# State reads and outputs of the SSD branch moved in front of adaLN units, with outputs cut into four column strips

## The chip, the cores and the metric

The kernel runs on one core of one Trainium2 chip. The metric is the device time of one execution in microseconds (us); less is better. All times below come from the hardware profiler's record of one execution, or from timed runs.

## The reference, cut to what matters

One layer of a decoder runs on 256 prompt tokens and 8 x 8 sample tokens (320 columns in all). The part that the change touches is the SSD branch (Mamba-2), in 8 groups of 8 heads:

```
cs = cumsum(dt * A)
cb = einsum('btgn,bsgn->btsg', C, B)               # products of one group
w  = cb * exp(cs_t - cs_s) * dt                     # weights, masked to s <= t
y  = einsum('btsgh,bsghp->btghp', w, x)             # outputs
y += exp(cs) * einsum('btgn,bghpn->btghp', C, h0)   # read of the old state h0
h  = exp(cs_last) * h0 + einsum('bsgh,bsghp,bsgn->bghpn', dL, x, B)   # new state
y  = rmsnorm_group((y + d_skip * x) * silu(z)) * ssd_norm
```

Beside it the adaLN modulation is computed: `mod = silu(c) @ w_ada`, for 9 rows (1 prompt, 8 samples), 12288 columns wide.

## The kernel before, in words

Every large product is a GEMM with fp32 weights that are split in two parts (`whi` by ScalarE at line 132, `wlo` by VectorE at line 106); a block of it is three TensorE matmuls (`hi*hi`, `lo*hi`, `hi*lo`) over 320 columns, called `mm` in the profile. `quad_mm` runs one quad, that is 512 x 512 weights: 2 halves of 4 output blocks (`mb`), 6 matmuls per block. The blocks of one GEMM lie in four PSUM banks (tag `mm`, 4 buffers), so the next GEMM's block takes the bank of the same block of the GEMM before it, once that has been evacuated.

TensorE's order is the order in which the program is written; the other engines get theirs from a scheduler when the program is built, and each engine then works strictly in that order. Two kinds of small work are put between the blocks:

- **Background generators.** `bg.tick()` is called after every block (8 times in a quad). A generator yields how many ticks it wants to skip. `ssd_work` is the one that matters: for each group it transposes B and x, reads the 8 sample states with `C` (`inter`: 4 matmuls for each half `hf`, each on a strip of 32 columns of the array, four strips side by side), updates the states (`upd`), makes the products (`cb`), token-major x (`xT`, then `xdt`), the weights (`w`: three Relu and one Exp on ScalarE, a product on GpSimd), the outputs (`y`: 8 matmuls for each of 4 steps `j`, on two strips of 64 columns), and the prompt's final state (`fin`). The decay rows `csb` (two loads of 640 KB) feed the weights.
- **adaLN units.** `ada.mm()` stands behind every second quad (`ada_every`). A unit is 4 matmuls on four strips of 32 columns (`ad`); when the unit before it closed a column block, `flush` first puts 4 transposes (`p`) in front of it.

One group takes, in this order: a GEMM for `xs` (with the convolution), one for the gate `z` (its four blocks go through a Silu on ScalarE in `evac_z`), then 4 GEMMs of one quad each for the projection of the group before (`w_sp`; evacuated by VectorE into `yb`). `ssd_work` begins when `z` begins: tick 16 is the end of z's second quad, tick 32 the end of z, tick 48 and 64 the ends of the second and fourth quads of the projection. An adaLN unit stands behind each of these four.

Before the change the generator goes by tick counts alone: the first read is at tick 16, the second at tick 26, the outputs at ticks 52, 57, 62 and 67. Both `csb` loads and four state loads are issued at tick 16.

Of the kernel before, what the change touches and what calls it, by code (L numbers as in the profile page):

```python
# [19 lines left out]
NT = 320  # L20
# [40 lines left out]
def hybrid_kernel(tc, ctx, a, o):  # L61
# [71 lines left out]
        return first, tt(eng, lo, src, hi.bitcast(F32), ALU.subtract)  # L133


    class Background:
        def __init__(self):
            self.queue = []
# [2 lines left out]
        def add(self, gen):  # L141
            self.queue.append(gen)

        def tick(self):
            if self.wait > 0:
                self.wait -= 1
                return
            if self.queue:
                try:
                    self.wait = next(self.queue[0]) or 0  # L150
                except StopIteration:
                    self.queue.pop(0)
# [95 lines left out]
    class Ada:  # L248
# [23 lines left out]
                self.loaded.append((c, b0, nb, q, raws))  # L272

        def mm(self):
            self.flush()
            if not self.loaded:
                return
            c, b0, nb, q, raws = self.loaded.pop(0)
            if q == 0:
                t = psum.tile([128, 512], F32, tag="ad", bufs=1, name="ad")  # L280
                self.ps = t
            w = 128 * nb
            m = 2048 // w
            n = m // len(raws)
            for j in range(m):
                T.matmul(self.ps[32 * (j % 4):32 * (j % 4) + 32, :w], c_s[:, m * q + j, :],
                         raws[j // n][:, (j % n) * w:(j % n) * w + w], start=q == 0 and j < 4,
                         stop=q == nb - 1 and j >= m - 4, tile_position=(0, 32 * (j % 4)))
            if q == nb - 1:
                part = stile([128, 512], name="adap")  # L290
                S.copy(part[:, :w], self.ps[:, :w])  # L291
                self.parts.append((c, b0, nb, part))
# [31 lines left out]
        T.matmul(ps, wh, xl, start=False, stop=False)  # L324
        T.matmul(ps, wl, xh, start=False, stop=stop)

    def quad_mm(pss, name, xq, first, last, evac, n_ada, apart, later):
        xh, xl = xq
        if n_ada:
            ada.load()  # L330
        for h in range(2):
            wh, wl = stream.take(name + (h,))
            for mb in range(4):
                for k2 in range(2):
                    kk = 2 * h + k2
                    c = k2 * 512 + mb * 128
                    block(pss[mb][:, :NT], wh[:, c:c + 128], wl[:, c:c + 128],
                          xh[:, kk], xl[:, kk], first and kk == 0, last and kk == 3)
                if mb == 0:
                    stream.ahead(1 if apart and last and h == 1 else S_AHEAD)  # L340
                if h == 0 and mb == 1 and later is not None:
                    later()
                if last and h == 1 and evac is not None:
                    evac(mb, pss)
                bg.tick()
        if n_ada:
            ada.mm()

# [3 lines left out]
    def gemm(names, quads, evac, apart=False):  # L352
        pss = [mm_ps() for _ in range(4)]
        n = len(names)
        for q in range(n):
            quad_no[0] += 1
            xq = quads(q) if callable(quads) else quads[q]
            quad_mm(pss, names[q], xq, q == 0, q == n - 1, evac,
                    1 if ada_every[0] and len(ada.units) > 4 and quad_no[0] % ada_every[0] == 0 else 0, apart,
                    (lambda: quads(q + 1)) if callable(quads) and q + 1 < n else None)  # L360


# [611 lines left out]
    def v8(x):  # L974
        return x.rearrange("p (h d) -> p h d", d=64)
# [4 lines left out]
    def ssd_work(W):  # L980
# [19 lines left out]
        xl = stile([64, 512], name="xl")  # L1000
        tt(V, v8(xl), v8(ps[0:64]), bc8(dtL_tok[:, hsl]), ALU.mult)
        tt(V, v8(xs_tok[0:64]), v8(ps[0:64]), bc8(dt_tok[0:64, 2, hsl]), ALU.mult)
        yield 4

        psA = ax_ps("inter")
        for hf in range(2):
            mv = stack_v(xl, hf)
            states.read(psA, [cpad[:, 4 * hf + j] for j in range(4)], hf, hf == 0, hf == 1)
            for j in range(4):
                st = states.tiles[4 * hf + j]  # L1010
                tt(G, v8(st), v8(st), bc8(ecs_all[:, hsl, 4 * hf + j]), ALU.mult)
            if hf == 0:
                csb = []
                for i in range(2):
                    t = qtile(name="csb")
                    src = bass.AP(tensor=cs_d.tensor, offset=cs_d.offset + (8 * g + 4 * i) * NT,
                                  ap=[[0, 128], [NT, 4], [1, NT]])
                    now(nc.sync.dma_start(t, src))
                    csb.append(t)
            yield 1  # L1020
            for j in range(4):
                states.update(hf, j, hst[hf][:, j], mv, lambda st, ps: tt(V, st, st, ps, ALU.add))
                yield 1
        inter = stile([128, 512], name="inter")
        tt(V, v8(inter), v8(psA), bc8(ecs_r[:, hsl]), ALU.mult)
        yield 1
        states.store(8)

        ps = ax_ps("cb")
        T.matmul(ps[:, 0:256], Bc[:, 0:128], Cc[:, 0:256], start=True, stop=True)  # L1030
        T.matmul(ps[:, 256:384], Bc[:, 128:256], Cc[:, 128:256], start=True, stop=True)
        wide = W.bcm.rearrange("p a b -> p (a b)")[:, NT * 2 * (g % 2) + NP:NT * 2 * (g % 2) + NP + 128]
        T.matmul(ps[:, 384:448], wide, Cc[:, 256:320], start=True, stop=True)
        cb = stile([128, 448], name="cb")
        tt(V, cb[:, 0:384], ps[:, 0:384], mask[:, 0:384], ALU.mult)
        tt(V, cb[0:64, 384:448], ps[0:64, 384:448], mask[0:64, 384:448], ALU.mult)

        wt = ws[0:64]
        for i in range(2):
            now(tt(V, wt[:, 4 * i:4 * i + 4], csb[i][0:64, :, NP:],  # L1040
                   cs_tok[0:64, 2, 8 * g + 4 * i:8 * g + 4 * i + 4].unsqueeze(2).to_broadcast([64, 4, 64]),
                   ALU.subtract))
        V.tensor_scalar(out=wt, in0=wt, scalar1=0.0, scalar2=None, op0=ALU.min)
        act(wt, wt, AF.Exp)
        tt(V, wt, wt, cb[0:64, 384:448].unsqueeze(1).to_broadcast([64, 8, 64]), ALU.mult)
        yield

        xdt = []
        for tb in range(2):
            ps = ax_ps("xT")  # L1050
            for mb in range(4):
                T.transpose(ps[:, 128 * mb:128 * mb + 128], xs[:, mb, 128 * tb:128 * tb + 128], ident)
            xt = stile([128, 512], name="xdt")
            tt(V, v8(xt), v8(ps), bc8(dt_tok[:, tb, hsl]), ALU.mult)
            xdt.append(xt)
            yield

        ps = ax_ps("bT")
        for tb in range(2):
            T.transpose(ps[:, 128 * tb:128 * tb + 128], Bc[:, 128 * tb:128 * tb + 128], ident)  # L1060
        bt = stile([128, 2, 128], name="bt")
        S.copy(bt, ps[:, 0:256].rearrange("p (a b) -> p a b", a=2))
        xL = []
        for tb in range(2):
            xl = stile([128, 512], name="xL")
            tt(G, v8(xl), v8(xdt[tb]), bc8(dL_tok[:, tb, hsl]), ALU.mult)
            xL.append(xl)
        yield 3
        ps = ax_ps("fin")
        for tb in range(2):  # L1070
            T.matmul(ps, bt[:, tb], xL[tb], start=tb == 0, stop=tb == 1)
            yield
        fs = stile([128, 512], name="fs")
        S.copy(fs, ps)
        nc.sync.dma_start(o["ssm_p"][g], fs)


        def weights(h):
            cbr = csb[h // 4][:, h % 4]
# [6 lines left out]
            tt(G, w, w, cb[:, 0:384], ALU.mult)  # L1086
            return w

        ahead = [weights(0), weights(1)]
        yield 4  # L1090
        for j in range(4):
            if j < 3:
                ahead += [weights(2 * j + 2), weights(2 * j + 3)]

            ps = ax_ps("y")
            w = [ahead.pop(0), ahead.pop(0)]
            for cols, lhs, rhs, first in (
                    (slice(0, 256), xdt[0], lambda e: w[e][:, 0:256], True),
                    (slice(128, 256), xdt[1], lambda e: w[e][:, 256:384], False),
                    (slice(256, 320), xs_tok, lambda e: ws[:, 2 * j + e], True),  # L1100
                    (slice(256, 320), inter, lambda e: sel, False)):
                for e in range(2):
                    h = 2 * j + e
                    T.matmul(ps[64 * e:64 * e + 64, cols], lhs[:, 64 * h:64 * h + 64], rhs(e), start=first,
                             stop=not first, tile_position=(0, 64 * e))
            i = 4 * g + j
            V.scalar_tensor_tensor(out=xs[:, j], in0=xs[:, j], scalar=vec[:, V_DS + i:V_DS + i + 1],
                                   in1=ps[:, :NT], op0=ALU.mult, op1=ALU.add)
            yield 4

    def ssd_finish(W):
        g, xs = W.g, W.xs
# [332 lines left out]
```

## Time and profile before

| | |
|---|---|
| median of 3 runs | 2912.64 us (2911.92 to 2913.28) |
| the profiled execution | 2912.8 us |
| its span, first to last instruction | 2910.7 us |
| TensorE matmuls busy | 2863.7 us, 98% of the span |
| VectorE, ScalarE, GpSimd busy | 1587.1, 1239.2, 378.3 us |
| SSD outputs (`y`) | from 726.9 to 1587.1 us of the span |

The span is 2.1 us shorter than the execution's own time. Matmul rows give a start, a length and a count; matmuls overlap, so what a stretch costs is read from starts: while only `mm` run, one starts every 0.147 us. "[0.98 <-DVE st L106]" behind a row is the time for which the engine was idle before it and the work that ended this.

### The profile page before, as it was taken

The page shows a single profiled execution, that of the slowest core. Times are in us where ns is not written, and L with a number is a line of the kernel's source. Part 1 is how long each engine was busy: PE and PEld are TensorE (multiplying, and loading weights), DVE is VectorE, ACT ScalarE, POOL GpSimd, SP SyncE. Part 2 cuts the span into 40 slices and gives each one's busy share as a digit, 9 for nine tenths or more (in the row PEclk, how much of TensorE's full clock was granted, in tenths as well). Part 3 has the DMA queues.
Part 4 walks back from the last instruction along what each step waited for, and adds up shares of the span by engine and source line. Part 5 has one row for each costly group of instructions (what it writes and reads, how often), then busy time and mean ns, then how long its engine had stood idle before and what let it go on. Part 6 is the DMA issues. An engine that isn't in the chain of part 4 may idle for free.

```text
span 2910.7 us, 48455 instructions
## 1 busy us (share of the span) xinstructions
PE 2863.7 (98%) x19596; PEld 2683.9 (92%) x19596; DVE 1587.1 (55%) x2302; ACT 1239.2 (43%) x1955; POOL 378.3 (13%) x517
## 2 busy tenths in 40 slices
PE   7999999999999999999999999999999999999998
PEld 5889999988889989889888999999999999999998
DVE  5666555666646666666665544456444444443445
ACT  4354544344454554445454333335333233333333
POOL 0012021123223232323232000000000000000000
PEclk9999999999999999999999999999999999999999
DMA  9855755747666676775767544554444444444443
GB/s 385 320 171 190 243 170 192 244 143 274 224 236 238 204 259 198 254 240 200 259 200 253 196 168 157 170 206 150 148 152 149 149 152 151 147 152 150 148 151 116
DMA packets 181111, 575.54 MB, mean 198 GB/s; under 512 B 23252, under 2 KB 24600, under 8 KB 180888
## 3 DMA queue, kind: packets, MB, share of 16 engines
q1 hardware_dynamic: 180888, 572.45, 57.8%
q8 instruction: 154, 2.52, 0.3%
q14 instruction: 69, 0.57, 0.1%
HBM read 528.63 MB, written 43.74 MB: 197 GB/s over the span
## 4 chain that ended last, share of the span: by engine, by line
PE 50%; DVE 1%; ACT 0%; issue 0%; DVEq 0%
PE mm L115 49%; PE ad L115 0%; DVE x L106 0%; PE y L115 0%; PE sum L115 0%; DVE x L1193 0%; PE upd L115 0%; PE fin L115 0%; PE inter L115 0%; PE xT L118 0%; PE p L118 0%; DVE ss L106 0%; PE cb L115 0%; DVE rt L106 0%; ACT adap L291 0%
## 5 line engine op out<-in xcount | busy, mean ns | idle before, releaser
L106 DVE TENSOR_TENSOR wlo<-raw,whi 128x1024 fp32r<-128x1024 f32 x712 | 884.3, 1244 | 949.6 <-ACT whi L132 946.5
L132 ACT CAST whi<-raw 128x1024 fp32r<-128x1024 f32 x712 | 745.7, 1048 | 1366.5 <-PE mm L115 1032.7
L115 PE MATMUL mm<-hh,whi 128*128 128x320 f32 x2560 | 817.6, 319 | 8.7 <-ACT u L946 6.7
L115 PE MATMUL mm<-hh,wlo 128*128 128x320 f32 x2560 | 793.2, 310 | 0.8 <-DVE wlo L106 0.8
L115 PE MATMUL mm<-hl,whi 128*128 128x320 f32 x2560 | 792.4, 310 | 1.3 <-DVE hl L106 1.3
L115 PEld LDWEIGHTS mm<-hh,whi 128*128 128x128 f32 x2560 | 482.9, 189 | 89.4 <-issue 42.5
L115 PEld LDWEIGHTS mm<-hl,whi 128*128 128x128 f32 x2560 | 483.3, 189 | 11.1 <-issue 3.8
L115 PEld LDWEIGHTS mm<-hh,wlo 128*128 128x128 f32 x2560 | 482.8, 189 | 1.4 <-DVE wlo L106 1.3
L115 PE MATMUL mm<-gh,whi 128*128 128x320 f32 x1408 | 435.3, 309 | 0.8 <-ACT gh L1267 0.8
L115 PE MATMUL mm<-gl,whi 128*128 128x320 f32 x1408 | 435.4, 309 | 0.0
L115 PE MATMUL mm<-gh,wlo 128*128 128x320 f32 x1408 | 435.1, 309 | 0.0
L115 PEld LDWEIGHTS mm<-gh,whi 128*128 128x128 f32 x1408 | 264.3, 188 | 1.8 <-ACT gh L1267 1.8
L115 PEld LDWEIGHTS mm<-gl,whi 128*128 128x128 f32 x1408 | 264.3, 188 | 0.5 <-DVE gl L106 0.3
L115 PEld LDWEIGHTS mm<-gh,wlo 128*128 128x128 f32 x1408 | 264.3, 188 | 0.0
L115 PE MATMUL mm<-ahi,whi 128*128 128x320 f32 x704 | 217.5, 309 | 0.0
L115 PE MATMUL mm<-alo,whi 128*128 128x320 f32 x704 | 217.5, 309 | 0.0
L115 PE MATMUL mm<-ahi,wlo 128*128 128x320 f32 x704 | 217.5, 309 | 0.0
L106 POOL TENSOR_TENSOR ss<-ss,sq 128x320 f32<-128x320 f32 x14 | 12.8, 912 | 1401.9 <-ACT sq L109 1401.8
L115 PE MATMUL mm<-yhi,whi 128*128 128x320 f32 x512 | 170.2, 332 | 0.0
L115 PE MATMUL mm<-yhi,wlo 128*128 128x320 f32 x512 | 158.4, 309 | 0.6 <-DVE wlo L106 0.6
L115 PE MATMUL mm<-ylo,whi 128*128 128x320 f32 x512 | 158.0, 309 | 0.0
L115 PEld LDWEIGHTS mm<-ahi,whi 128*128 128x128 f32 x704 | 132.1, 188 | 0.0
(281 smaller groups left out, 3616.0 us busy)
## 6 DMA issues: line engine op xcount, KB each, us to landing
raw<-w_in SPq DMA_DIRECT2D x320, 512.0 KB, 4.1
raw<-w_fi SPq DMA_DIRECT2D x176, 512.0 KB, 3.3
raw<-w_ada SPq DMA_DIRECT2D x120, 512.0 KB, 5.7
raw<-w_fo SPq DMA_DIRECT2D x88, 512.0 KB, 3.4
raw<-w_sp SPq DMA_DIRECT2D x64, 512.0 KB, 5.3
araw<-w_ada SPq DMA_DIRECT2D x52, 512.0 KB, 8.5
st<-S_gla SPq DMA_DIRECT2D x64, 256.0 KB, 5.1
gla_s<-st SPq DMA_DIRECT2D x64, 256.0 KB, 4.6
```

Source lines behind the costliest of these rows:

```text
L106: return eng.tensor_tensor(out=out, in0=in0, in1=in1, op=op)
L115: Tensor.last = nc.tensor.matmul(*args, **kw)
L132: first = S.copy(hi, src)
```

## The change

A tick that stands right in front of an adaLN unit is now marked as such (`unit`), and a generator can yield `UNIT` to skip to it. In `ssd_work` both state reads and the outputs (two steps `j` together) wait for such a tick: ticks 16, 32, 48 and 64. An output matmul is cut into two of 32 columns, so that one step is 16 matmuls over four strips. `ada.mm` runs its unit first and the transposes of the block before it afterwards. The products `cb`, the token-major x and the first two heads' weights stand between the two reads (ticks 24 to 29), the sample weights and heads 2 and 3 at tick 42, heads 4 to 7 behind the first outputs. `fin` stands behind the first outputs. States 4 to 7 are loaded at tick 13, `csb` at ticks 20 and 32.

```diff
+    UNIT = "unit"
...
-        def tick(self):
-            if self.wait > 0:
+        def tick(self, unit=False):
+            if self.wait == UNIT and not unit:
+                return
+            if self.wait != UNIT and self.wait > 0:
                 self.wait -= 1
                 return
...
         def mm(self):
+            old, self.parts = self.parts, []
+            self.unit()
+            new, self.parts = self.parts, old
             self.flush()
+            self.parts = new
...
-    def quad_mm(pss, name, xq, first, last, evac, n_ada, apart, later):
+    def quad_mm(pss, name, xq, first, last, evac, slot, apart, later):
+        n_ada = slot and len(ada.units) > 4
...
-                bg.tick()
+                bg.tick(h == 1 and mb == 3 and slot)
...
+        mv = stack_v(xl, 0)
+        yield 1
+        states.load(8)
+        yield UNIT
+        psA = ax_ps("inter")
+        for hf in range(2):
+            states.read(psA, [cpad[:, 4 * hf + j] for j in range(4)], hf, hf == 0, hf == 1)
+            for j in range(4):
+                st = states.tiles[4 * hf + j]
+                tt(G, v8(st), v8(st), bc8(ecs_all[:, hsl, 4 * hf + j]), ALU.mult)
+            if hf == 1:
+                decay_rows(1)
+            yield 1
+            for j in range(4):
+                if hf == 0 and j == 1:
+                    decay_rows(0)
+                states.update(hf, j, hst[hf][:, j], mv, lambda st, ps: tt(V, st, st, ps, ALU.add))
+                if j < 3:
+                    yield 1
+            if hf == 0:
+                cb = products()
+                yield 1
+                for tb in range(2):
+                    token_major(tb)
+                    yield tb
+                ahead += [weights(h) for h in range(2)]
+                mv = stack_v(xl, 1)
+                yield UNIT
...
+        states.store(8)
+        sample_weights()
+        ahead += [weights(h) for h in range(2, 4)]
...
+        for p in range(2):
+            yield UNIT
+            for j in (2 * p, 2 * p + 1):
...
+                    for e in range(2):
+                        for c in (0, 32):
+                            at = 64 * e + c
+                            T.matmul(ps[at:at + 32, cols], lhs[:, 128 * j + at:128 * j + at + 32], rhs(e),
+                                     start=first, stop=not first, tile_position=(0, at))
...
+            if p == 0:
+                ahead += [weights(h) for h in range(4, 8)]
+                yield 3
```

On TensorE, this is an output step of the last group before the change (`w` on `xdt`, `ws` and `inter` are its operands), alone between blocks of the projection:

```order
L115 MATMUL mm<-yhi,wlo 128x320
L115 MATMUL y<-w,xdt 64x256 x2
L115 MATMUL y<-w,xdt 64x128 x2
L115 MATMUL y<-ws,xs_tok 64x64 x2
L115 MATMUL y<-cst,inter 64x64 x2
L115 MATMUL mm<-yhi,whi 128x320
```

And the last outputs of the same group in the changed program, two steps and the unit:

```order
L115 MATMUL mm<-yhi,wlo 128x320
L115 MATMUL y<-w,xdt 32x256 x4
L115 MATMUL y<-w,xdt 32x128 x4
L115 MATMUL y<-ws,xs_tok 32x64 x4
L115 MATMUL y<-cst,inter 32x64 x4
L115 MATMUL y<-w,xdt 32x256 x4
L115 MATMUL y<-w,xdt 32x128 x4
L115 MATMUL y<-ws,xs_tok 32x64 x4
L115 MATMUL y<-cst,inter 32x64 x4
L115 MATMUL ad<-raw,c_s 32x512 x4
L115 MATMUL mm<-hh,whi 128x320
```

Four lone steps became two pairs, and each pair touches a unit; a step has twice the matmuls.

On ScalarE, this is the end of the z GEMM in the seventh group before the change (`z<-mm` are the four Silu evacuations, `whi` the weight casts, `adap` a unit's result):

```order
L132 CAST whi<-raw 128x1024 x2
L109 ACTIVATE z<-mm 128x320 x2
L132 CAST whi<-raw 128x1024
L109 ACTIVATE z<-mm 128x320 x2
L132 CAST whi<-raw 128x1024
L291 COPY adap<-ad 128x512
L132 CAST whi<-raw 128x1024 x2
L109 ACT_TABLE_LOAD
L109 ACTIVATE ws<-ws 64x512
```

And the same place in the changed program (`w` are the weights of heads 0 and 1):

```order
L132 CAST whi<-raw 128x1024
L109 ACTIVATE z<-mm 128x320
L109 ACTIVATE w<-csb,cs_tok 128x128
L109 ACTIVATE w<-csb,nd_tok 128x128
L109 ACTIVATE w<-csb,cs_tok 128x128 x2
L109 ACT_TABLE_LOAD
L109 ACTIVATE w<-w 128x384
...
L519 CAST mv<-xl 32x512
L109 ACTIVATE w<-w 128x384
L109 ACT_TABLE_LOAD
L109 ACTIVATE z<-mm 128x320 x3
L301 COPY adap<-ad 128x512
```

The work for two heads' weights, with a table load at either end, now stands between the first and the second Silu of z. The order is the same in all 8 groups. In the whole program ScalarE has 61 table loads, 45 before.

On VectorE, the same group in the changed program between its two reads; `st` is a state's addition of `upd`, which frees the bank that `upd` wrote:

```order
L106 TENSOR_TENSOR st<-st,upd 128x512
L106 TENSOR_TENSOR wlo<-raw,whi 128x1024
L106 TENSOR_TENSOR st<-st,upd 128x512
L106 TENSOR_TENSOR wlo<-raw,whi 128x1024
L106 TENSOR_TENSOR st<-st,upd 128x512 x2
L106 TENSOR_TENSOR cb<-cb,cst 128x384
```

Before the change no `wlo` stands between the four `st` of this read, and `cb` comes after the second read's.

## Rows read from the trace of the kernel before

**Rows 1.** The page, busy time of each engine (share of span, instructions).
```profile
PE 2863.7 (98%) x19596; PEld 2683.9 (92%) x19596; DVE 1587.1 (55%) x2302; ACT 1239.2 (43%) x1955; POOL 378.3 (13%) x517
```
**Rows 2.** Chain that ended last, in order of time: start, us, what.
```profile
1433.90 1.76 PE mm L115 x12
...
1457.09 0.44 PE p L118 x4
```
**Rows 3.** Timeline of TensorE around a lone state read (left out) at 1430.64.
```profile
1430.40 0.31 PE L115 MATMUL mm<-hh,wlo 128*128 128x320 f32 x1
...
1431.89 0.30 PE L115 MATMUL mm<-hl,whi 128*128 128x320 f32 x1
```
**Rows 4.** Timeline of TensorE, a state read with a unit right behind it.
```profile
1418.03 0.31 PE L115 MATMUL mm<-hh,wlo 128*128 128x320 f32 x1
1418.27 1.06 PE L115 MATMUL inter<-st,cpad 128*32 128x512 f32 x8
1419.15 1.04 PE L115 MATMUL ad<-raw,c_s 128*32 128x512 f32 x8
...
1420.37 0.31 PE L115 MATMUL mm<-hl,whi 128*128 128x320 f32 x1
```
**Rows 5.** Timeline of TensorE: read, four transposes and unit between these two.
```profile
1524.28 0.31 PE L115 MATMUL mm<-hh,wlo 128*128 128x320 f32 x1
...
1527.35 0.31 PE L115 MATMUL mm<-hl,whi 128*128 128x320 f32 x1
```
**Rows 6.** Timeline of TensorE, one output step on two strips.
```profile
1461.92 0.31 PE L115 MATMUL mm<-yhi,wlo 128*128 128x320 f32 x1
...
1462.86 0.28 PE L115 MATMUL y<-ws,xs_tok 128*64 128x64 f32 x4
1462.97 0.29 PE L115 MATMUL y<-cst,inter 128*64 128x64 f32 x4
...
1463.45 0.31 PE L115 MATMUL mm<-ylo,whi 128*128 128x320 f32 x1
```
**Rows 7.** Timeline of ScalarE, a cast and the Silu of z behind it.
```profile
1436.03 1.04 ACT L132 CAST whi<-raw 128x1024 fp32r<-128x1024 f32 x1
1436.97 0.44 ACT L109 ACTIVATE z<-mm 128x320 f32<-128x320 f32 x1
```
**Rows 8.** Timeline of ScalarE, a copy for `mv`; Relus and Exp of weights.
```profile
1419.69 0.62 ACT L508 CAST mv<-xl 32x512 fp32r<-32x512 f32 x1
...
1455.84 0.41 ACT L109 ACTIVATE w<-csb,cs_tok 128x128 f32<-128x128 f32 x1
...
1457.02 0.51 ACT L109 ACTIVATE w<-w 128x384 f32<-128x384 f32 x1
```
**Rows 9.** Timeline of ScalarE, a table load between a cast and Silus.
```profile
776.79 1.05 ACT L132 CAST whi<-raw 128x1024 fp32r<-128x1024 f32 x1 [2.31 <-DMA raw<-w_in]
777.86 1.28 ACT L109 ACT_TABLE_LOAD   x1
779.15 1.02 ACT L109 ACTIVATE xs<-cacc 128x256 f32<-128x256 f32 x4
```
**Rows 10.** Timeline of TensorE, first block behind a late evacuation.
```profile
632.50 0.64 PE L115 MATMUL mm<-hh,whi 128*128 128x320 f32 x1 [6.66 <-ACT u L946]
```
**Rows 11.** Groups by line and shape, `upd`: busy, mean ns, idle before.
```profile
L115 PE MATMUL upd<-mv,hs 96*128 96x512 f32 x128 | 52.4, 410 | 4.0 <-DVE st L106 2.6 <-DVE mv L106 1.1 <-DVE st L670 0.3
```
**Rows 12.** Stretches: us, TensorE busy (instructions), granted clock, DMA share, GB/s.
```profile
210.95:214.39 3.44, 2.34 (x11) 1.00 1.02 375
214.39:217.80 3.41, 3.41 (x13) 0.50 0.63 205
...
796.50:799.90 3.40, 2.42 (x17) 1.00 1.05 405
798.80:802.20 3.40, 3.39 (x22) 1.00 0.99 358
```
**Rows 13.** Who waited for whom: total us, times, longest.
```profile
ACT whi L132 <- DMA raw<-w_sp: 44.6, 35, 4.4
```

More of the change, by code (lines that the diff above doesn't have):

```diff
@@ L274, in mm, with unit @@
         def mm(self):
+            old, self.parts = self.parts, []
+            self.unit()
+            new, self.parts = self.parts, old
             self.flush()
+            self.parts = new
+        def unit(self):
             if not self.loaded:
@@ L358, in gemm @@
             quad_mm(pss, names[q], xq, q == 0, q == n - 1, evac,
-                    1 if ada_every[0] and len(ada.units) > 4 and quad_no[0] % ada_every[0] == 0 else 0, apart,
+                    ada_every[0] > 0 and quad_no[0] % ada_every[0] == 0, apart,
                     (lambda: quads(q + 1)) if callable(quads) and q + 1 < n else None)
@@ L1002, in ssd_work @@
         tt(V, v8(xs_tok[0:64]), v8(ps[0:64]), bc8(dt_tok[0:64, 2, hsl]), ALU.mult)
[L1003 to L1049, printed above, removed]
+        csb, xdt, ahead = [], [], []
+        def products():
+            ps = ax_ps("cb")
+            T.matmul(ps[:, 0:256], Bc[:, 0:128], Cc[:, 0:256], start=True, stop=True)
+            T.matmul(ps[:, 256:384], Bc[:, 128:256], Cc[:, 128:256], start=True, stop=True)
+            wide = W.bcm.rearrange("p a b -> p (a b)")[:, NT * 2 * (g % 2) + NP:NT * 2 * (g % 2) + NP + 128]
+            T.matmul(ps[:, 384:448], wide, Cc[:, 256:320], start=True, stop=True)
+            cb = stile([128, 448], name="cb")
+            tt(V, cb[:, 0:384], ps[:, 0:384], mask[:, 0:384], ALU.mult)
+            tt(V, cb[0:64, 384:448], ps[0:64, 384:448], mask[0:64, 384:448], ALU.mult)
+            return cb
@@ new lines, in sample_weights @@
+        def sample_weights():
+            wt = ws[0:64]
+            for i in range(2):
+                now(tt(V, wt[:, 4 * i:4 * i + 4], csb[i][0:64, :, NP:],
+                       cs_tok[0:64, 2, 8 * g + 4 * i:8 * g + 4 * i + 4].unsqueeze(2).to_broadcast([64, 4, 64]),
+                       ALU.subtract))
+            V.tensor_scalar(out=wt, in0=wt, scalar1=0.0, scalar2=None, op0=ALU.min)
+            act(wt, wt, AF.Exp)
+            tt(V, wt, wt, cb[0:64, 384:448].unsqueeze(1).to_broadcast([64, 8, 64]), ALU.mult)
@@ L1050, in ssd_work, with token_major @@
+        def token_major(tb):
             ps = ax_ps("xT")
@@ L1055, in ssd_work, with weights, decay_rows @@
             xdt.append(xt)
-            yield
+        def weights(h):
+            cbr = csb[h // 4][:, h % 4]
+            hh = 8 * g + h
+            w = pool.tile([128, 384], F32, tag="w", bufs=4, name="w")
+            now(act(w[:, 0:128], cbr[:, 0:128], AF.Relu, scale=-1.0, bias=cs_tok[:, 0, hh:hh + 1]))
+            now(act(w[:, 128:256], cbr[:, 128:256], AF.Relu, scale=-1.0, bias=nd_tok[:, hh:hh + 1]))
+            now(act(w[:, 256:384], cbr[:, 128:256], AF.Relu, scale=-1.0, bias=cs_tok[:, 1, hh:hh + 1]))
+            act(w, w, AF.Exp, scale=-1.0)
+            tt(G, w, w, cb[:, 0:384], ALU.mult)
+            return w
+        def decay_rows(i):
+            t = qtile(name="csb")
+            src = bass.AP(tensor=cs_d.tensor, offset=cs_d.offset + (8 * g + 4 * i) * NT,
+                          ap=[[0, 128], [NT, 4], [1, NT]])
+            now(nc.sync.dma_start(t, src))
+            csb.append(t)
+        mv = stack_v(xl, 0)
[26 more added lines that the diff above has]
+                yield UNIT
+        inter = stile([128, 512], name="inter")
+        tt(V, v8(inter), v8(psA), bc8(ecs_r[:, hsl]), ALU.mult)
+        yield 1
+        states.store(8)
+        sample_weights()
+        ahead += [weights(h) for h in range(2, 4)]
         ps = ax_ps("bT")
@@ L1067, in ssd_work @@
             xL.append(xl)
[L1068 to L1079, printed above, removed]
-            hh = 8 * g + h
-            w = pool.tile([128, 384], F32, tag="w", bufs=4, name="w")
-            now(act(w[:, 0:128], cbr[:, 0:128], AF.Relu, scale=-1.0, bias=cs_tok[:, 0, hh:hh + 1]))
-            now(act(w[:, 128:256], cbr[:, 128:256], AF.Relu, scale=-1.0, bias=nd_tok[:, hh:hh + 1]))
-            now(act(w[:, 256:384], cbr[:, 128:256], AF.Relu, scale=-1.0, bias=cs_tok[:, 1, hh:hh + 1]))
-            act(w, w, AF.Exp, scale=-1.0)
-            tt(G, w, w, cb[:, 0:384], ALU.mult)
-            return w
@@ L1089, in ssd_work @@
[L1089 to L1109, printed above, removed]
+        for p in range(2):
+            yield UNIT
+            for j in (2 * p, 2 * p + 1):
+                ps = ax_ps("y")
+                w = [ahead.pop(0), ahead.pop(0)]
+                for cols, lhs, rhs, first in (
+                        (slice(0, 256), xdt[0], lambda e: w[e][:, 0:256], True),
+                        (slice(128, 256), xdt[1], lambda e: w[e][:, 256:384], False),
+                        (slice(256, 320), xs_tok, lambda e: ws[:, 2 * j + e], True),
+                        (slice(256, 320), inter, lambda e: sel, False)):
+                    for e in range(2):
[3 more added lines that the diff above has]
+                                     start=first, stop=not first, tile_position=(0, at))
+                i = 4 * g + j
+                V.scalar_tensor_tensor(out=xs[:, j], in0=xs[:, j], scalar=vec[:, V_DS + i:V_DS + i + 1],
+                                       in1=ps[:, :NT], op0=ALU.mult, op1=ALU.add)
+            if p == 0:
+                ahead += [weights(h) for h in range(4, 8)]
+                yield 3
+                ps = ax_ps("fin")
+                for tb in range(2):
+                    T.matmul(ps, bt[:, tb], xL[tb], start=tb == 0, stop=tb == 1)
+                    yield
+                fs = stile([128, 512], name="fs")
+                S.copy(fs, ps)
+                nc.sync.dma_start(o["ssm_p"][g], fs)
@@ L1111, in ssd_finish @@
+        yield 1
     def ssd_finish(W):
```

## The prediction

> **What bounds the kernel now.** I read the page's busy times first: TensorE is busy for 98% of the span [rows 1], so time comes only out of what TensorE does or waits for. Next the chain that ended last: twelve `mm` take 1.76 us [rows 2], 0.147 us each. That is the yardstick for the timeline of TensorE: between the last `mm` start ahead of some small work and the second `mm` start behind it lie two such steps and the price of the small work. (The second, because the first one behind a strip starts early and is long.)
>
> - A lone state read: 1431.89 - 1430.40 - 0.29 = 1.20 us [rows 3].
> - A read with a unit right behind it: 1420.37 - 1418.03 - 0.29 = 2.05 us [rows 4]. A lone unit has the read's shape and I price it the same, 1.20, so two apart cost 2.40: standing together saves 0.35. The second one adds 0.85, which is what its streaming takes; the 0.35 is paid on entering and leaving the strips.
> - Read, four transposes, unit: 1527.35 - 1524.28 - 0.29 = 2.78 us [rows 5]. With the transposes (0.44 [rows 2]) behind instead it would be 2.49: 0.29 less.
> - A lone output step on two strips: 1463.45 - 1461.92 - 0.29 = 1.24 us [rows 6].
>
> **The change, part by part.**
>
> *Outputs.* A step streams 256, 128, 64 and 64 columns, twice over on each pair of strips before, once on each of four now, so every strip streams what it streamed before: 512 columns, as a read does. Inside a cluster of strips I therefore price a step at the 0.85 of the added unit [rows 4], plus 0.02 for its eight short rounds: 0.87. It saves 1.24 - 0.87 = 0.37, and there are 8 groups x 4 steps: **-11.8 us**. Lower bound of the saving: the four small matmuls of a row on two strips come 0.11 us apart (1462.86 to 1462.97), 0.028 each [rows 6]; if that is a pace of instructions and not of streaming, the small ones of a step (8 matmuls, two passes each) now take 16 x 0.028 = 0.45 instead of 0.22, 0.23 x 32 = 7 us given back. I take the streaming price, because 0.028 is also what 64 columns on two strips need.
>
> The Trainium skill speaks against the cut too: "TensorE: Matmul & The Clock Gate", section "Wait — 56ns, not 53.3ns?", states that matmuls never start less than about 25 ns apart, however small. By that, those 16 would take at least 0.40 us, and the sum would be 6 us worse. No row here tells whether that holds across strips.
>
> *Reads.* The second read of each group goes from lone to touching a unit: 8 x 0.35 = -2.8. The first already touches a unit in 4 groups; in the other 4 the transposes stood between: 4 x 0.29 = -1.2. Together **-4.0 us**. Elsewhere `flush` behind the unit instead of ahead only swaps neighbours; ahead of the FFN two units that stood together get transposes between them, +0.3.
>
> *Weights of heads 0 and 1.* Here TensorE gets a new wait. In ScalarE's new order they stand, with two table loads, between the first and second Silu of z. Take m0 as the start of the last matmul of z's first block. ScalarE: the cast ahead of the first Silu takes the buffer of the half that ended one block (0.88) before m0, so it starts at m0 - 0.88 + 0.31 (that matmul's length) + 0.05, and the Silu follows a cast by 1436.97 - 1436.03 = 0.94 [rows 7]: m0 + 0.42. Then: Silu 0.44; four Relus 1457.02 - 1455.84 = 1.18; table load 1.28; Exp 0.51; two Relus 0.59; the `mv` copy 0.62; Exp 0.51; table load 1.28; second Silu 0.44 [rows 7 to 9]. That is 6.85; less about 0.15 where neighbours overlap (a Relu is 0.41 long and starts every 0.30), 6.7. So z's second bank is free at m0 + 7.1. TensorE: three more blocks, read and unit together, and the first block of the projection: (18 + 1 + 6) x 0.147 + 2.05 = m0 + 5.72. There the second block needs that bank: a wait of 1.4, and 0.1 for the weight load that no longer overlaps, 1.5 us. In 8 groups: **+12 us**. That such a wait does hold TensorE is shown where a convolution's evacuation came late: 6.66 us [rows 10]. Lower bound: 0.9 each, if the copy and a Relu overlap fully. Upper bound: the cast in front may itself wait for its weights; casts waited 44.6 us for `w_sp`, 1.27 each in the mean [rows 13], which would make it 2.8 each, 22 us.
>
> What is queued behind: z's third and fourth Silu are ready in time, since TensorE needs them 0.88 apart and ScalarE delivers 0.34 apart. VectorE waits for the `mv` copy, with the next `wlo` behind it; the raw buffer that this frees, and on SP's queue the weights and second `csb` load behind that, come some 5 us later than they could. `csb` is needed 14 us later, which covers it; the projection's first evacuations stand behind a `wlo` made from those weights and have, by my sum, some 0.2 us to spare.
>
> The Trainium skill has a dearer switch: "ScalarE: Activation LUTs", section "What ACT_TABLE_LOAD costs", counts about 1.38 us of drain beside the 1.28 of the load. The trace disagrees: the load begins 0.02 behind a cast's end and a Silu starts 0.01 behind the load [rows 9]. By the page each wait would be 2.8 us longer and the sum 22 us worse.
>
> *Products and spread loads.* `cb` now comes right behind the fourth update, while the read still holds one of three banks (`ax`); it needs the third state's addition, behind which no slack is left if a `wlo` is late. `upd` waited 2.6 us for the same reason [rows 11]; the loads that made `wlo` late there are spread now, but the room is smaller. I let the two cancel: 0, with bounds -2.6 and +5.6 (0.7 in each group). GpSimd's and VectorE's work is the same; the weights of heads 2 to 7 fall into stretches in which, by the same row lengths, they are ready about 1 us before the outputs.
>
> **Sum:** -11.8 - 4.0 + 0.3 + 12.0 + 0 = -3.5 us against the profiled execution's 2912.8 (span 2910.7), which is 0.2 above the median of the runs: **2909 us**. What a measurement of this kernel can tell from no change is 0.2%, 5.8 us, so the likeliest case reads "same" more often than not.
>
> **The rivals.**
>
> 1. *The wait at z is hidden* (the evacuation comes in time all the same). Then -15.5: 2897. For it: ScalarE is busy for only 43% of the span [rows 1]; against it: its order is fixed, and the lengths in it add up.
> 2. *Weights come late around z*, and the wait grows to 2.8 in each group, or the projection's own evacuations wait as well: +10 on the sum, 2919. For it: the 44.6 us [rows 13]; against it: both `csb` and four state loads are moved out of this burst, where DMA was full (1.05 [rows 12]).
> 3. *The clock falls behind the new wait; slower.* A stretch of 3.44 us in which TensorE was busy for 2.34 was followed by 3.41 at a granted clock of 0.50, the 1.2 GHz level; another, busy for 2.42 of 3.40, was not, and 2.4 GHz went on [rows 12]. The new wait, 1.5 long, comes near both. At half clock 3.41 us give half the work, 1.7 lost; in all 8 groups +13.6, or 2923. It decides (slower by over 5.8) from 6 groups on.
> 4. *Small matmuls go by their number:* +7, 2916.
> 5. *A table switch holds ScalarE for longer than its row says.* If each cost its 1.28 once more, every wait would be 2.6 longer and the time 2909 + 21 = 2930. Against it: the gaps of 0.02 and 0.01 around the load [rows 9].
>
> **How the numbers follow.** Chances: my sum 0.50, rival 1 0.12, rival 2 0.16, rival 3 0.10, rival 4 0.10, rival 5 0.02. The sum's own range is 2903 to 2916 (wait of 0.9 to 1.8 in each group, -2.6 to +4 for `cb`). Some 0.30 of it lies below 2906.8 and 0.04 above 2918.5. Faster by over 0.2%: 0.15 + 0.12 + 0.01 = 0.28. Slower: 0.02 + 0.10 + 0.08 + 0.02 + 0.02 = 0.24. Same: 0.48. The range takes in rivals 1 to 3 for the most part: 2898 to 2922.
>
> **What would show it.** In the timeline of TensorE after the change: two output steps and a unit in 2.9 to 3.0 us by the same measure (much more: rival 4); read and unit always 2.05; idle of 1.2 to 1.5 us ahead of the projection's second block, ended by ScalarE's `z` (none: rival 1). Between z's first and second Silu the two table loads, 6.3 us. In stretches behind that wait the granted clock: 1.00 (0.50: rival 3). I would be wrong if TensorE waits somewhere in these groups that I count as covered: at `cb` for `st`, at the projection's next quad for `yb`, at the outputs for `w`.

## Result: slower by 1%, and the profile after

Changed kernel: **2940.23 us** median of 4 runs (2935.61 to 2948.33). Before, on the same chip: 2912.96 (2911.92 to 2914.30). Ratio 1.0096, 95% interval 1.0083 to 1.0109. The forecast was 2909, range 2898 to 2922.

The profiled execution took 2939.63 us, its span is 2937.8: 27.1 more than before. Busy times after the change, to be held against [rows 1]:

```profile
PE 2860.5 (97%) x20108; PEld 2686.8 (91%) x20108; DVE 1586.3 (54%) x2302; ACT 1263.0 (43%) x1971; POOL 360.3 (12%) x517
```

TensorE is busy for 3.2 us less in a span that is 27.1 longer, so it waits. The view of waits says for whom; TensorE's lines (engine, line, waited for: us in total, times, longest):

```profile
PE y L115 <- POOL w L106: 15.8, 7, 3.0
PE mm L115 <- ACT z L109: 15.5, 8, 2.6
...
PE cb L115 <- DVE st L106: 2.7, 3, 1.1
```

The second row was forecast (12). The first was not: in 7 of 8 groups the first outputs wait for weights that GpSimd has not finished. Gone in turn are the 2.6 us of `upd` for `st` [rows 11] and 1.4 for `wlo`.

One group, timeline of ScalarE, GpSimd, VectorE and TensorE ahead of its first outputs (start, length, instruction, count, [idle before <- what ended it]):

```profile
1327.73 1.05 ACT L132 CAST whi<-raw 128x1024 fp32r<-128x1024 f32 x1 [5.00 <-DMA raw<-w_sp]
...
1329.98 1.28 ACT L109 ACT_TABLE_LOAD   x1
...
1333.07 0.52 ACT L109 ACTIVATE w<-w 128x384 f32<-128x384 f32 x1
...
1331.88 1.02 POOL L106 TENSOR_TENSOR w<-w,cb 128x384 f32<-128x384 f32 x1 [10.61 <-ACT w L109]
1332.86 2.50 POOL L106 TENSOR_TENSOR xL<-xdt,dL_tok 128x512 f32<-128x512 f32 x2
1335.31 1.97 POOL L106 TENSOR_TENSOR w<-w,cb 128x384 f32<-128x384 f32 x1
...
1328.81 1.23 DVE L106 TENSOR_TENSOR wlo<-raw,whi 128x1024 fp32r<-128x1024 f32 x1 [1.90 <-ACT whi L132]
...
1334.57 1.87 DVE L106 TENSOR_TENSOR wlo<-raw,whi 128x1024 fp32r<-128x1024 f32 x1
...
1332.97 0.31 PE L115 MATMUL mm<-yhi,wlo 128*128 128x320 f32 x1
...
1334.11 0.60 PE L115 MATMUL y<-w,xdt 128*32 128x256 f32 x4
1337.34 0.63 PE L115 MATMUL y<-w,xdt 128*32 128x256 f32 x8 [2.63 <-POOL w L106]
...
1339.84 0.31 PE L115 MATMUL mm<-ylo,whi 128*128 128x320 f32 x1
```

ScalarE stood 5.00 us at a cast whose raw weights had not landed; the weights of heads 2 and 3 are queued behind it, with a table load. Head 3's Exp ended at 1333.59, but GpSimd had by then begun the two `xL` products, which the final state needs much later. Head 3's product began only at 1335.31, and it took 1.97 instead of 1.02, beside a `wlo` of VectorE. The second output step had begun on head 2's strips at 1334.11 and stood until 1337.34. By the prediction's measure the cluster (two steps, unit and transposes) cost 1339.84 - 1332.97 - 0.29 = 6.58; 3.34 is its price without a wait (experiment 3). So the wait of 2.63 cost 3.24. In the other three groups in which the clock did not fall in this cluster it also costs 0.6 more than its wait. I read these 0.6 as two strips that run alone, first head 2's and then head 3's; no run tests that by itself.

The wait at z in another group, ScalarE, then TensorE:

```profile
1199.06 1.05 ACT L132 CAST whi<-raw 128x1024 fp32r<-128x1024 f32 x1 [0.22 <-DMA raw<-w_sp]
1200.13 0.44 ACT L109 ACTIVATE z<-mm 128x320 f32<-128x320 f32 x1
...
1201.75 1.28 ACT L109 ACT_TABLE_LOAD   x1
...
1204.82 0.52 ACT L109 ACTIVATE w<-w 128x384 f32<-128x384 f32 x1
1205.36 1.28 ACT L109 ACT_TABLE_LOAD   x1
1206.65 1.09 ACT L109 ACTIVATE z<-mm 128x320 f32<-128x320 f32 x3
...
1207.14 0.41 PE L115 MATMUL mm<-yhi,whi 128*128 128x320 f32 x1 [2.18 <-ACT z L109]
```

From the first Silu's start to the second's end (1206.65 + 0.44) are 6.96 us, in all 8 groups within 0.01. The cast ahead of the first Silu waited 0.14 to 0.38 us, in four groups last for raw weights (as here) and in four until a matmul had ended.

The clock: stretches (the busy time of TensorE, of its weight loads, VectorE, ScalarE and GpSimd, then the granted clock, DMA share, GB/s). The first three begin 0.3 to 1.5 us behind the end of a wait (of 2.37, 2.10 and 1.69), the last right behind the one of 2.63 above:

```profile
1226.86:1230.27 3.41, 3.41 (x17) 2.34 (x10) 0.38 (x1) 2.17 (x7) 3.41 (x5) 0.50 0.55 171
708.04:711.45 3.41, 3.41 (x15) 3.31 (x14) 1.82 (x3) 0.81 (x2) 0.58 (x1) 0.50 1.04 368
1458.97:1462.38 3.41, 3.41 (x14) 3.31 (x13) 1.47 (x2) 1.71 (x3) 2.16 (x3) 0.50 0.84 258
1337.34:1340.75 3.41, 3.41 (x48) 2.49 (x49) 2.40 (x4) 3.41 (x12) 3.41 (x3) 1.00 0.56 195
```

Between 640 and 1620 us of the span five stretches of 3.41 us ran at a granted clock of 0.50, the 1.2 GHz level; before the change none did.

### The profile page after: what moved, and what is told of

Its sections match the earlier page's. It is cut to its first block, busy times and chain, and to the rows that moved or that the text cites. A ratio compares the mean times of both kernels' runs of the same rounds, so it can differ in the third digit from the quotient of the medians.

```text
span 2937.8 us, 49525 instructions
## 1 busy us (share of the span) xinstructions
PE 2860.5 (97%) x20108; PEld 2686.8 (91%) x20108; DVE 1586.3 (54%) x2302; ACT 1263.0 (43%) x1971; POOL 360.3 (12%) x517
## 4 chain that ended last, share of the span: by engine, by line
PE 69%; issue 2%; POOL 2%; DVE 2%; DMA 2%; ACT 2%; DVEq 0%; ACTq 0%; POOLq 0%; SPq 0%
PE mm L115 64%; PE ad L115 2%; DMA raw<-w_in 1%; POOL w L106 1%; PE y L115 1%; POOL xL L106 1%; ACT whi L132 1%; POOL st L106 1%; PE fin L115 0%; DMA raw<-w_sp 0%; DVE wlo L106 0%; ACT L109 0%; ACT w L109 0%; PE inter L115 0%; DVE cacc L966 0%
```

## The experiments

Ratios are to the kernel before, on the same chip: 2912.6 us beside experiments 1, 2, 3 and 5, 2913.2 beside 4, 6, 7 and 8 (medians of 23 and 22 runs). The changed kernel itself was timed beside 2912.96, so differences to its 2940.23 compare two chips.

**1. `xL` behind the weights of head 3** (on GpSimd alone; ScalarE's order stays).

```diff
-            tt(G, v8(xl), v8(xdt[tb]), bc8(dL_tok[:, tb, hsl]), ALU.mult)
...
                 ahead += [weights(h) for h in range(4, 8)]
+                for tb in range(2):
+                    xl = stile([128, 512], name="xL")
+                    now(tt(G, v8(xl), v8(xdt[tb]), bc8(dL_tok[:, tb, hsl]), ALU.mult))
+                    xL.append(xl)
```

> The two products xL on GpSimd are put behind the weights of head 3 instead of between those of heads 2 and 3; nothing else moves on ScalarE. My theory: the 15.8 us that the first outputs wait for GpSimd's weights come from these 2.5 us, and the three half-clock stretches behind those waits (1.7 us lost in each) follow from the waits. So the waits fall to under 4 us in all, the half-clock stretches that are new fall from five to two, the waits at z stay at 15.5: 2940 - 12 - 5 = 2923 us (2918 to 2928). Rival 1: ScalarE's chain for these weights is what is late, and xL only fills the gap: the waits lose under a third, 2934 to 2940. Rival 2: the half-clock stretches don't hang on the waits: five stay, 2928.

2919.36 us; ratio 1.0020 (1.0011 to 1.0029). Its waits:

```profile
PE mm L115 <- ACT z L109: 16.2, 8, 3.1
...
PE y L115 <- POOL w L106: 0.6, 2, 0.4
```

The outputs' wait is gone, though the cast ahead of heads 2 and 3 still waits up to 5.55 us for raw weights: ScalarE's chain is late, but not too late, and rival 1 falls. Four half-clock stretches are left instead of two, three of them where TensorE resumes behind a wait at z and one behind a wait of 1.77 at `cb`, so that on the clock neither theory's count came out.

**2. Weights of heads 0 and 1 behind z.**

```diff
             if hf == 1:
                 decay_rows(1)
+                ahead += [weights(h) for h in range(2)]
...
-                ahead += [weights(h) for h in range(2)]
                 mv = stack_v(xl, 1)
                 yield UNIT
```

> The weights of heads 0 and 1 are made behind the second read and so behind all four Silus of z; xL stays where it is. My theory: the waits at z (15.5 us) and the two half-clock stretches behind them (3.4) go, ScalarE's table loads fall from 61 to 45, and the waits of the first outputs stay about as long (12 to 20 us): 2940 - 19 = 2921 us (2914 to 2928). Rival: the wait only changes its place, because four heads' weights now stand in ScalarE's queue behind z: the first outputs wait 30 us or more in all, 2936 to 2942.

2918.40 us; ratio 1.0015 (1.0006 to 1.0023). TensorE's waits at z are gone, and those of the outputs are as long as they were, `xL` being still in the way:

```profile
PE y L115 <- POOL w L106: 15.4, 8, 2.9
```

ScalarE has 16 table loads fewer (39 instead of 55 at line 109). The wait did not change its place: the rival falls (new are 1.9 us of waits for `ya` and `yb`). Two half-clock stretches are left, behind the two longest waits (2.71 and 2.92).

**3. Both.**

> Both edits together. My theory: all that made the change slower is the waits at z, the waits of the first outputs and the half-clock stretches behind them, 15.5 + 15.8 + 8.5 us; with most of them gone the savings of the reads and outputs show: 2904 us (2897 to 2912), below the 2913 of the kernel before. Rival: with four heads' weights behind z the outputs still wait 1.5 us or more in each group, 2918 to 2930, above it.

**2897.58 us; ratio 0.9951 (0.9940 to 0.9963)**: faster than before. The two edits gave 20.9 and 21.8 alone, 42.7, and 42.65 together. In the view of waits neither is left beyond some tenths, no half-clock stretch stands between 640 and 1620 us, and what is left of the new waits is

```profile
PE cb L115 <- DVE st L106: 3.1, 5, 1.5
```

Here a cluster can be priced without a wait: two steps and unit (1321.73 to 1324.96), and two steps, unit and transposes (1302.60 to 1306.23). The last three rows are a first cluster that did lose time:

```profile
1321.73 0.31 PE L115 MATMUL mm<-yhi,wlo 128*128 128x320 f32 x1
1321.97 0.86 PE L115 MATMUL y<-w,xdt 128*32 128x256 f32 x16
1322.64 0.29 PE L115 MATMUL y<-ws,xs_tok 128*32 128x64 f32 x8
1322.75 0.29 PE L115 MATMUL y<-cst,inter 128*32 128x64 f32 x8
1322.87 0.83 PE L115 MATMUL y<-w,xdt 128*32 128x256 f32 x16
...
1324.96 0.30 PE L115 MATMUL mm<-hl,whi 128*128 128x320 f32 x1
...
1302.60 0.31 PE L115 MATMUL mm<-yhi,wlo 128*128 128x320 f32 x1
...
1305.58 0.66 PE L118 MATMUL p<-erl,adap 128*128 128x128 f32 x4
...
1306.23 0.30 PE L115 MATMUL mm<-ylo,whi 128*128 128x320 f32 x1
...
1060.31 0.31 PE L115 MATMUL mm<-yhi,wlo 128*128 128x320 f32 x1
...
1061.44 1.29 PE L115 MATMUL y<-w,xdt 128*32 128x256 f32 x12
...
1064.21 0.31 PE L115 MATMUL mm<-ylo,whi 128*128 128x320 f32 x1
```

1324.96 - 1321.73 - 0.29 = 2.94, so with 1.20 for the first of three, a step adds 0.87. With transposes 1306.23 - 1302.60 - 0.29 = 3.34. But 1064.21 - 1060.31 - 0.29 = 3.61: in three of the 8 groups the first cluster cost 3.61, 3.50 and 3.97 where 2.94 is the price, 2.3 us in all, while the view of waits has one wait of 0.4 there. While two strips are still busy, TensorE is not idle, and that view counts idle time alone.

**4. `cb` a block later, on top of both.**

```diff
+                yield
                 cb = products()
-                yield 1
+                yield
```

> As the run with both edits, and the products cb of a group stand one block of projection work (0.88 us) behind the fourth update instead of right behind it. Theory: cb waits for the addition of an earlier state, 3.1 us over 5 groups in that run, longest 1.5; a block of 0.88 later, under 1 us of it is left: 2897.6 - 2.5 = 2895 us (2892 to 2898). Rival: the addition comes late because VectorE waits for weights, so that the wait stays or comes back at the transposes behind it: 2897 to 2899.

**2894.40 us; ratio 0.9934 (0.9922 to 0.9946)**, the lowest median; its interval overlaps that of experiment 3. The wait that was left is now

```profile
PE cb L115 <- DVE st L106: 0.5, 2, 0.3
```

The waits for `yb` rose from 0.4 to 1.1. In the two profiles the last `mm` starts at 2876.97 (experiment 3) and 2876.91 us, so that the profiles do not show the gain that the medians suggest: that the wait went is shown, that the kernel became faster by it is not.

**5. The changed kernel with outputs on two strips.**

```diff
-                        for c in (0, 32):
-                            at = 64 * e + c
-                            T.matmul(ps[at:at + 32, cols], lhs[:, 128 * j + at:128 * j + at + 32], rhs(e),
...
+                        at = 64 * e
+                        T.matmul(ps[at:at + 64, cols], lhs[:, 128 * j + at:128 * j + at + 64], rhs(e),
...
```

> The changed kernel with its output steps on two strips of 64 columns, as before, but at their new places: two steps with a unit right behind them. Theory 1, as I priced it: what saves is four strips, and a step on two costs 1.24 us also in a cluster: cluster 3.7 instead of 2.94 us, +11.8, 2952 us. Theory 2: what saves is the company: each strip streams 512 columns either way and the 0.37 is the price of entering and leaving strips, paid once in a cluster: cluster 2.9 to 3.1, 2940 us.

2941.23 us (2936.42 to 2964.31); ratio 1.0115 (1.0089 to 1.0141): not to be told from the changed kernel. Its cluster:

```profile
1357.90 0.31 PE L115 MATMUL mm<-yhi,wlo 128*128 128x320 f32 x1
1358.14 0.87 PE L115 MATMUL y<-w,xdt 128*64 128x256 f32 x8
...
1360.06 1.06 PE L115 MATMUL ad<-raw,c_s 128*32 128x512 f32 x8
...
1361.30 0.31 PE L115 MATMUL mm<-hl,whi 128*128 128x320 f32 x1
```

1361.30 - 1357.90 - 0.29 = 3.11: 0.17 more than on four strips, 0.085 a step. Theory 2 holds: of the 0.37 that a step saves, 0.28 comes from standing together and 0.085 from the cut (2.7 us in the kernel). All 8 last clusters of this profile cost 3.11.

**6. The kernel before with four strips alone.**

```diff
-                    T.matmul(ps[64 * e:64 * e + 64, cols], lhs[:, 64 * h:64 * h + 64], rhs(e), start=first,
...
+                    for c in (0, 32):
+                        T.matmul(ps[64 * e + c:64 * e + c + 32, cols], lhs[:, 64 * h + c:64 * h + c + 32], rhs(e),
...
```

> The kernel before, with its output steps, each alone at its old place, on four strips of 32 columns instead of two of 64. By the run of the changed kernel on two strips four strips are worth 0.085 us in each of 32 steps: a lone step falls from 1.24 to 1.15 to 1.22 us, 2912.6 - 1 to - 3 = 2911 us, not to be told from no change. Rival: twice as many instructions cost more than the strips give back when nothing stands beside them: a step of 1.3 us or more, 2915 or more.

2907.96 us; ratio 0.9982 (0.9973 to 0.9991). A lone step:

```profile
1564.43 0.31 PE L115 MATMUL mm<-yhi,wlo 128*128 128x320 f32 x1
1564.67 0.86 PE L115 MATMUL y<-w,xdt 128*32 128x256 f32 x16
...
1565.93 0.31 PE L115 MATMUL mm<-ylo,whi 128*128 128x320 f32 x1
```

1565.93 - 1564.43 - 0.29 = 1.21 against 1.24 [rows 6]: about 1 us in 32 steps; the rival falls. The time fell by some 4 us more. In this profile `upd` waits 1.4 for `st` (2.6 before), nothing waits 1.4 for `wlo`, and the half-clock stretch at 214 us [rows 12] is missing, 1.7. That stretch comes and goes with one and the same program: of the two profiles of the changed kernel the first lacks it and the second has it, at 213.77. Why the waits fell, I did not settle.

**7. Weights of heads 0 and 1 ahead of z**, with `xL` as in experiment 1.

```diff
                 cb = products()
+                ahead += [weights(h) for h in range(2)]
                 yield 1
...
-                ahead += [weights(h) for h in range(2)]
                 mv = stack_v(xl, 1)
```

> As the run with xL behind the weights of head 3, and the weights of heads 0 and 1 are written right behind the products cb, so that they stand ahead of z's first Silu on ScalarE instead of between the first and the second. The same work, and as many table loads or more. Theory: the waits at z come from where this work stands, not from how much it is or from the number of table loads: 16.2 us of waits there fall under 3, and the half-clock stretches with them: 2919 - 13 - 5 = 2901 us (2895 to 2907). Rival 1: the row of decays that these weights read lands late, and holds ScalarE's casts and with them TensorE: a new wait of 1 us or more in each group, 2908 to 2930. Rival 2: table loads themselves hold up the Silus of z wherever they stand: 2915 to 2920.

2921.59 us; ratio 1.0027 (1.0018 to 1.0036). My theory was right on z and wrong on the time. Waits, TensorE's and one of ScalarE's:

```profile
PE y L115 <- POOL w L106: 10.5, 16, 0.9
...
PE mm L115 <- ACT z L109: 0.8, 2, 0.6
...
ACT w L109 <- DMA csb<-cs_d: 33.9, 8, 5.2
```

With as many table loads as the changed kernel (55), z waits 0.8 us instead of 16.2 in experiment 1: it is the place that counts (rival 2 falls). But ScalarE now stands 33.9 us for the decay rows (rival 1). That casts and raw buffers, and so the next weights, are late behind it I read from rows only: a cast ahead of heads 2 and 3 waits up to 7.3 us for raw `w_sp` (up to 6.0 in experiment 3), and TensorE then waits twice in each group at the outputs.

**8. Both `csb` loads together again, on top of both edits.**

```diff
-            if hf == 1:
-                decay_rows(1)
+            if hf == 0:
+                decay_rows(0)
+                decay_rows(1)
...
-                if hf == 0 and j == 1:
-                    decay_rows(0)
```

> As the run with both edits, but the two loads of decay rows issued together behind the first read, as before the change, instead of spread. My prediction counted the spreading of loads at nothing: 2897.6, within 3 us. Rival: spread loads keep raw weights and with them wlo in time; together, they bring back waits at upd and cb as before the change, over 4 us in all beside the 3.1 at cb: 2901 or more.

2898.02 us; ratio 0.9949 (0.9936 to 0.9962): the same as spread. The waits at `cb` are gone, one at `yb` (1.6) and two at `wlo` (0.6) stand there: the rival falls, and loads that stand together do not by themselves bring back the waits at `upd`.

**9. The changed kernel, a second profile.**

> The changed kernel once more, for a second profile of the same program. Theory: the waits at z and at the first outputs belong to the program and stand at the same matmuls with the same lengths within 0.3 us (15.5 and 15.8 in all, give or take 2), but whether the clock falls behind one of them differs from execution to execution: three to eight half-clock stretches, not all behind the same waits; time 2935 to 2948. Rival: each wait above some length is followed by a half-clock stretch and no other is, so that the stretches stand at the same five places.

2941.68 us, a single run (the kernel before beside it: 2910.69). The waits return, the clock differs:

```profile
PE mm L115 <- ACT z L109: 16.0, 8, 3.3
PE y L115 <- POOL w L106: 15.9, 6, 3.0
```

Two stretches of it, columns as above, and the rows of the waits at either:

```profile
1073.93:1077.34 3.41, 3.17 (x11) 3.07 (x12) 0.68 (x2) 1.78 (x4) 2.38 (x3) 0.50 0.89 321
1464.76:1468.17 3.41, 3.41 (x22) 3.32 (x23) 1.82 (x2) 2.41 (x5) 1.60 (x2) 1.00 0.95 267
...
1074.17 0.64 PE L115 MATMUL mm<-yhi,whi 128*128 128x320 f32 x1 [2.05 <-ACT z L109]
...
1464.76 0.42 PE L115 MATMUL mm<-yhi,whi 128*128 128x320 f32 x1 [2.56 <-ACT z L109]
```

Six half-clock stretches in or behind 14 waits of over 1 us; in the first profile five behind 17. The stretch at 1073.93 begins 0.24 us before the end of a wait of 2.05; the wait of 2.56 that ended at 1464.76 was followed by none. The first profile has the same: 1.69 with a stretch behind it, 2.63 and 2.57 without. So length alone does not decide, and the rival falls. Single waits moved by more than the 0.3 that I expected (z in one group: 1.69 and 2.56).

## Why the prediction was wrong

**The step that failed**: "the weights of heads 2 to 7 fall into stretches in which, by the same row lengths, they are ready about 1 us before the outputs". I added up ScalarE's rows and neither looked at GpSimd's new order, where `xL` stands between heads 2 and 3 for 2.5 us, nor at the cast ahead of them, which waits 5 us for raw weights. (That cast waits as long in experiments 1 and 3, and there the outputs hardly wait: what cost the time is `xL`.) The prediction named "at the outputs for `w`" as a place that would refute it, and had neither rival nor price for it. I counted it at nothing; it cost 15.8 us of waits and by the clusters above some 0.6 in each of 7 groups besides (experiment 1: 20.9 with the clock).

Longer rows on GpSimd came on top. Head 3's product took 1.97 us beside a `wlo`, where head 2's took 1.02; that `wlo` took 1.87, the one at 1328.81 took 1.23. The Trainium skill, "SBUF — State Buffer", section "Who interferes with whom", says that a VectorE instruction with two SBUF inputs contends with a GpSimd instruction that reads SBUF, and that the order of issue decides which of the two blocks. These rows agree: the `wlo` that began while an `xL` ran is 0.64 longer, the product that began while this `wlo` ran is 0.95 longer.

**The other terms**, predicted and measured, in the profiled span:

| term | predicted | measured |
|---|---|---|
| outputs | -11.8 | -11.8 (0.87 a step, clusters of 2.94) |
| reads | -4.0 | -4.0 (read and unit 2.05, with transposes 2.44) |
| FFN units | +0.3 | not looked at alone |
| wait at z | +12 | +15.5, and 0.1 behind each: 16.3 |
| first outputs' weights | 0 | +15.8, and 7 x 0.6: 20 |
| products and loads | 0 | +2.7 at `cb`, -2.6 and -1.4 of old waits: -1.3 |
| clock | 0 | five stretches x 1.7, less the one at 214 us: +6.8 |

They add up to +26.3 of the 27.1, which is closer than it deserves. Read from the starts of the same `mm` in both profiles, 26.4 us arise between 614 and 1700 us, where the table has 28.0 (without the stretch at 214). Up to 614 us the changed kernel is 1.1 ahead: this execution lacks that stretch, which comes and goes without the change (experiment 6). Behind the last `mm` it takes 1.7 longer; that piece lies between 15.5 and 17.4 us in all profiles, and I have no cause for it.

- *Wait at z*: right mechanism, too small. My 6.7 us between first Silu and free bank are 6.96, and the first Silu, which I had 0.42 us behind m0 (the last matmul of z's first block) in every group, came 0.39 to 1.43 behind it. Where it came at 0.39 the wait was 1.53; in four of the other six groups the cast ahead of it waited last for raw weights: rival 2, in small. Experiments 2 and 7 show that the place of the weights causes it.
- *Outputs*: the size was right, and so was the split into 0.35 for entering and leaving strips and the rest for streaming: by it a lone step on four strips costs 1.22, and experiment 6 has 1.21. What I had not said is that the saving needs the company, hardly the cut (experiment 5).
- *Rival 4* falls: sixteen small matmuls pass between 1322.64 and 1322.87, 0.014 us each. The Trainium skill, "TensorE: Matmul & The Clock Gate", section "Wait — 56ns, not 53.3ns?", states a least distance of about 25 ns between starts; across strips these rows disagree.
- *Rival 5* falls: the load at 1205.36 began 0.02 behind an Exp's end, the Silu 0.01 behind the load. The Trainium skill, "ScalarE: Activation LUTs", section "What ACT_TABLE_LOAD costs", counts about 1.38 us of drain for a switch; these rows have no room for it.
- *Rival 3*: in part. The clock fell behind the new waits, those at the outputs included, but behind about one in three, and cost 5 x 1.7 = 8.5 us and not 13.6.
- *Rival 1* gave 2897 for the gains alone. With the waits taken out the kernel runs in 2897.58: the gains were there, and were spent on two waits for other engines. That the two numbers agree to 0.6 us is in part luck: in experiment 3 waits at `cb` and first clusters cost 5.4 us, and old waits of 4.0 and the stretch at 214 are gone.

## What to carry to other kernels

When work is moved, write down the new queue of every engine that feeds it, up to the instruction that TensorE waits for: here the loss that I had not forecast stood on GpSimd, whose work had not changed at all, only its order. Work that nobody needs soon (`xL`, a weight for later) must not stand ahead of the last piece that the next cluster needs, nor between two evacuations. And a kernel at 98% busy pays for a wait more than its length: strips that run alone, and now and then a stretch at half the clock.

## What the runs showed of the hardware that I had not expected

- A step alone on four strips costs 1.21 us and on two 1.24; beside others 0.87 and 0.955. What costs is going over from full matmuls to strips and back (1.21 - 0.87 = 0.34 and 1.24 - 0.955 = 0.285), hardly the number of strips.
- Half-clock stretches between 640 and 1620 us: 5, 6, 4, 2, 7 and 2 in the profiles with many waits (changed kernel twice, experiments 1, 2, 5 and 7), none in experiments 3, 4 and 8, where no wait in these groups was over 1.7 us and few over 0.5. In experiment 7 they begin inside clusters that waited three times, none of these for as much as 1 us; other clusters that waited three times had none. With the same program they fall behind other waits in another execution; the runs of the changed kernel spread over 13 us, those of experiment 4 over 3.
